# Six raw weight buffers, five pairs of split weights, and one look-ahead of five parts

## The chip, the cores and the metric

The kernel runs on one core of a Trainium2 chip. The metric is the device time of one execution in microseconds, as the median of several runs. Beside the times there is one profiled execution, with a row for every instruction and transfer.

## The reference

A decoder trunk of four layers on one sequence of 256 tokens of width 1024, in float32. Layer by layer the token mixer is native sparse attention (NSA), MoBA block attention, a short gated convolution, and NSA again; each layer ends in a SwiGLU feed-forward network with 2816 hidden columns.

```python
def swiglu(a, w_gate, w_up, w_down):
    return (jax.nn.silu(a @ w_gate) * (a @ w_up)) @ w_down

def reference(x, ...):
    h = x
    for i in range(DEPTH):                      # DEPTH = 4
        kind, j = i % N_MIXERS, i // N_MIXERS   # 0 NSA, 1 MoBA, 2 short conv
        a = rms_norm(h, norm_mix[i])
        m = ...mixer of this kind...
        h = h + m
        a = rms_norm(h, norm_ffn[i])
        h = h + swiglu(a, ffn_w_gate[i], ffn_w_up[i], ffn_w_down[i])
    return rms_norm(h, norm_final)
```

## The kernel before

All weight matrices lie in memory as one long stream of blocks, in the order of use. A block, called a part, is 128 partitions x 1024 values (512 KB): eight 128x128 tiles. SyncE issues the load of a part (L113) into a tile named raw, of which there are RAW_BUFS. TensorE multiplies at float32r precision, so each float32 operand is split in two: ScalarE casts raw to the high half (L167, whi), VectorE subtracts the high half from raw to get the low half (L171, wlo; in a few places GpSimd, called POOL, does it in four pieces), and the product is hi x hi + hi x lo + lo x hi. A pair of whi and wlo occupies one of W_BUFS slots until TensorE has done its last multiplication with it; a raw buffer is free when its subtraction is done. One raw buffer is 4 KB of each partition and one pair 8 KB.

`take` hands out tiles in the order of the stream. When it is called for a part, it first writes down the loads and splits of the parts ahead of it that have none yet. How far ahead is AHEAD = 5 parts, and one more where the part in hand belongs to the feed-forward network (names "ffn" and "fast"). A scheduler then sets the order of instructions on each engine, from the order in which they were written and from the buffers that they need; each engine works its own list strictly in order, and SyncE's list is also the queue of loads and moves. So an engine that waits for one thing holds up all that stands behind it in its list.

The hidden columns are made in groups of four 128-column tiles (g = 0, 4, 8, 12, 16, 20). An ordinary group multiplies eight parts (L461 to L463). Groups g = 8 and g = 16 of each layer are "fast": the first half of the inner dimension goes through seven block products in place of eight. Their operands are the blocks B11, B21, B22 and the sums T1 to T4, which VectorE makes in place in the blocks (L120); the loads are at L130, the splits at L134 (shi, ScalarE) and L135 (slo, VectorE). The seven products (L401 to L403) run in the order B11, T1, B21, T2, B22, T4, T3. The number behind shi and slo counts operands in the order of use; the number behind raw, whi and wlo is the part's place in memory.

ScalarE's copies (L412) of three of the partial results, named gu, ph and u2/u3 (tile pr), empty the banks for use again: u3 is the last, made when all seven products are done. Then four ordinary raw parts, k = 4 to 7, are multiplied (L435 to L437) on top, into the same banks. So the first matmul of L435 into u3's bank waits for u3's copy.

What a group leaves goes through `hidden`: silu on ScalarE (L360), a product (L361) and a transpose (L362) on VectorE, then `spread`: 16 moves from SBUF to SBUF on SyncE's queue (L376, four at a time, tied behind the newest weight load), a cast (L257, ScalarE) and a subtraction (L258, VectorE) for each of the four tiles. In a fast group these last two belong to the group before the previous one, and `hidden` to the previous one.

In attention, scores are exponentiated on ScalarE (L581), the reciprocal of their sum comes from VectorE (rc, L583), POOL scales by it (pr, L585), and TensorE transposes the result (L659 and L661 in MoBA).

Of the kernel before, what the change touches and what calls it, by code (L numbers as in the profile page):

```python
# [27 lines left out]
PART = 8  # L28
LAYERS = range(4)
AHEAD = 5  # L30
RAW_BUFS = 4
W_BUFS = 6
PR_BUFS = 4
MOVES = 4
FF_BUFS = 26
# [28 lines left out]
class Kernel:  # L64
# [44 lines left out]
    def load_part(self, q, cut=1):  # L109
        t = self.wp.tile([P, PART * P], F32, tag="raw", name=f"raw{q}", bufs=RAW_BUFS)  # L110
        n = PART * P // cut
        for i in range(cut):
            self.load = self.nc.sync.dma_start(t[:, i * n:(i + 1) * n], self.ap["w"][q, :, i * n:(i + 1) * n])  # L113
        self.raw[q] = t
# [8 lines left out]
    def fast_part(self, x):  # L123
# [7 lines left out]
        b = self.blocks  # L131
        hi = self.operands.tile([P, PART * P], F32R, tag="whi", name=f"shi{x}", bufs=W_BUFS)
        lo = self.operands.tile([P, PART * P], F32R, tag="wlo", name=f"slo{x}", bufs=W_BUFS)
        self.nc.scalar.copy(hi, b[what])  # L134
# [10 lines left out]
    def split_part(self, x):  # L145
# [5 lines left out]
        if self.names[q] == "F":  # L151
            t = self.operands.tile([P, PART * P], F32, tag="whi", name=f"wf{q}", bufs=W_BUFS)
            nc.sync.dma_start(t, self.ap["w"][q])
# [4 lines left out]
        src = self.raw.pop(q)  # L158
        hi = self.operands.tile([P, PART * P], F32R, tag="whi", name=f"whi{q}", bufs=W_BUFS)
        lo = self.operands.tile([P, PART * P], F32R, tag="wlo", name=f"wlo{q}", bufs=W_BUFS)  # L160
        lo_eng, hi_eng = (e.get(self.names[q], d) for e, d in ((LO, "v"), (HI, "a")))
# [12 lines left out]
    def take(self, n=1):  # L174

        q, o = divmod(self.pos, PART)
        assert o + n <= PART
        ahead = AHEAD + (self.names[self.seq[q][0]] in ("ffn", "fast"))
        for x in range(q, min(q + ahead, len(self.seq))):
            if x not in self.parts:  # L180
                self.split_part(x)
        while self.jobs and self.jobs[0][0] <= self.when[q]:
            self.jobs.pop(0)[1]()
        self.pos += n
        hi, lo = self.parts[q]
        return hi[:, o * P:(o + n) * P], lo[:, o * P:(o + n) * P]
# [836 lines left out]
    def run(self):  # L1023
# [8 lines left out]
        for k in range(0, KT, 2):  # L1032
            nc.sync.dma_start(x[:, k:k + 2, :], ap["xt"][:, k:k + 2, :])
            q = k // 4
            if k % 4 == 0:
                self.raw[q] = self.wp.tile([P, PART * P], F32, tag="raw", name=f"raw{q}", bufs=RAW_BUFS)
            c = slice(k % 4 // 2 * n, (k % 4 // 2 + 1) * n)
            nc.sync.dma_start(self.raw[q][:, c], ap["w"][q, :, c])
        for q in range(2, RAW_BUFS):
            self.load_part(q)  # L1040
# [148 lines left out]
```

## Time and profile before

| | before |
|---|---|
| median of 3 runs | 1254.41 us (1254.0 to 1258.1) |
| profiled execution | 1258.91 us, of which the span is 1257.1 us |
| mean granted TensorE clock | 0.992 |
| TensorE busy | 1222.2 us (97%) |
| VectorE busy | 972.3 us (77%) |
| ScalarE busy | 718.0 us (57%) |
| POOL busy | 296.5 us (24%) |
| read from memory | 213.33 MB, 171 GB/s over the span |

Rows of the profile give the start and length of an instruction, its engine (PE is TensorE, DVE VectorE, ACT ScalarE, SP SyncE), its line, and out<-in tiles with buffer numbers left out; "[2.83 <-DMA pt<-pt]" means that the engine was idle for 2.83 us just before and that a move ended the wait. A row of waits gives the total, the count and the longest. Matmul rows overlap, since TensorE is pipelined: their pace is the distance between starts, 0.23 us for 512 columns at the full clock.

### The profile page before, as it was taken

The page shows a single profiled execution, that of the slowest core. Times are in us where ns is not written, and L with a number is a line of the kernel's source. Part 1 is how long each engine was busy: PE and PEld are TensorE (multiplying, and loading weights), DVE is VectorE, ACT ScalarE, POOL GpSimd, SP SyncE. Part 2 cuts the span into 40 slices and gives each one's busy share as a digit, 9 for nine tenths or more (in the row PEclk, how much of TensorE's full clock was granted, in tenths as well). Part 3 has the DMA queues.
Part 4 walks back from the last instruction along what each step waited for, and adds up shares of the span by engine and source line. Part 5 has one row for each costly group of instructions (what it writes and reads, how often), then busy time and mean ns, then how long its engine had stood idle before and what let it go on. Part 6 is the DMA issues. An engine that isn't in the chain of part 4 may idle for free.

```text
span 1257.1 us, 19456 instructions
## 1 busy us (share of the span) xinstructions
PE 1222.2 (97%) x6740; PEld 1055.8 (84%) x6740; DVE 972.3 (77%) x1741; ACT 718.0 (57%) x1290; POOL 296.5 (24%) x405
## 2 busy tenths in 40 slices
PE   8998999999999899999999999999999999999997
PEld 7987888878899788888888888878899878888786
DVE  7779897975868688887778898775758798879653
ACT  5689655644456445655444556464536896566442
POOL 1077650100113442000123250000330776400000
PEclk9999999999999999999999999999999999999999
DMA  8742166567654436766765655566666422664672
GB/s 296 232 148 95 68 219 184 166 184 222 233 172 141 159 106 188 247 208 209 226 220 170 197 177 176 174 214 181 223 219 207 136 78 76 207 193 154 209 233 83
DMA packets 91587, 227.21 MB, mean 181 GB/s; under 512 B 17504, under 2 KB 38368, under 8 KB 91488
## 3 DMA queue, kind: packets, MB, share of 16 engines
q1 hardware_dynamic: 91056, 225.41, 56.9%
q8 instruction: 53, 0.87, 0.3%
q10 hardware_dynamic: 432, 0.56, 0.1%
q14 instruction: 46, 0.38, 0.1%
HBM read 213.33 MB, written 1.05 MB: 171 GB/s over the span
## 4 chain that ended last, share of the span: by engine, by line
PE 48%; DVE 9%; ACT 3%; issue 3%; POOL 2%; DMA 2%; SPq 1%; POOLq 0%; ACTq 0%; DVEq 0%
PE psA L218 8%; PE psA L222 4%; DVE wlo L171 3%; PE psB L461 2%; PE psB L463 2%; PE psB L462 2%; PE psA L461 2%; PE psA L463 2%; PE psA L462 2%; SPq L376 1%; PE psB L218 1%; DMA raw<-in_w 1%; ACT whi L167 1%; PE psB L782 1%; PE psA L198 1%
## 5 line engine op out<-in xcount | busy, mean ns | idle before, releaser
L171 DVE TENSOR_TENSOR wlo<-raw,whi 128x1024 fp32r<-128x1024 f32 (+1 forms) x334 | 411.3, 1249 | 139.8 <-ACT whi L167 134.2
L167 ACT CAST whi<-raw 128x1024 fp32r<-128x1024 f32 (+1 forms) x347 | 357.1, 1039 | 283.7 <-DMA raw<-in_w 188.0
L218 PE MATMUL psA<-ff,whi 128*128 128x512 f32 x686 | 182.2, 393 | 0.2 <-DVE row L989 0.2
L218 PEld LDWEIGHTS psA<-ff,whi 128*128 128x128 f32 x686 | 124.5, 189 | 23.0 <-DVE row L989 0.6
L198 PE MATMUL psA<-at,whi 128*128 128x256 f32 x352 | 102.1, 290 | 1.7 <-DVE row L548 1.7
L222 PE MATMUL psA<-ff,wlo 128*128 128x256 f32 x686 | 101.4, 283 | 0.0
L222 PEld LDWEIGHTS psA<-ff,wlo 128*128 128x128 f32 x686 | 96.1, 191 | 5.3
L200 PE MATMUL psA<-at,wlo 128*128 128x256 f32 x352 | 100.6, 286 | 0.0
L199 PE MATMUL psA<-at,whi 128*128 128x256 f32 x352 | 100.4, 285 | 0.0
L585 POOL TENSOR_SCALAR pr<-pr,rc,gates 128x256 f32<-128x256 f32 (+1 forms) x128 | 72.2, 580 | 118.7 <-DVE rc L583 116.5
L461 PE MATMUL psB<-whi,at 128*128 128x512 f32 x224 | 87.9, 392 | 0.6 <-ACT pr L360 0.6
L463 PE MATMUL psB<-whi,at 128*128 128x512 f32 x224 | 87.3, 390 | 0.0
L461 PE MATMUL psA<-whi,at 128*128 128x512 f32 x224 | 87.3, 390 | 0.0
L463 PE MATMUL psA<-whi,at 128*128 128x512 f32 x224 | 87.3, 390 | 0.0
L462 PE MATMUL psB<-wlo,at 128*128 128x512 f32 x224 | 87.2, 390 | 0.0
L462 PE MATMUL psA<-wlo,at 128*128 128x512 f32 x224 | 87.2, 389 | 0.0
L285 POOL TENSOR_TENSOR ssq<-ssq,row 128x256 f32<-128x256 f32 x42 | 38.7, 922 | 205.5 <-ACT row L283 143.1
L171 POOL TENSOR_TENSOR wlo<-raw,whi 128x256 fp32r<-128x256 f32 x96 | 74.7, 812 | 38.2 <-ACT whi L167 17.2
L134 ACT CAST shi<-B 128x1024 fp32r<-128x1024 f32 x56 | 57.8, 1049 | 37.3 <-DVE B L120 25.3
L581 ACT ACTIVATE pr<-pr,mn 128x128 f32<-128x128 f32 (+1 forms) x160 | 71.2, 447 | 7.2 <-DVE mn L578 6.7
L135 DVE TENSOR_TENSOR slo<-B,shi 128x1024 fp32r<-128x1024 f32 x56 | 66.8, 1217 | 8.1 <-ACT shi L134 8.1
L198 PEld LDWEIGHTS psA<-at,whi 128*128 128x128 f32 x352 | 68.1, 193 | 2.7 <-DVE row L548 2.5
(293 smaller groups left out, 2720.2 us busy)
## 6 DMA issues: line engine op xcount, KB each, us to landing
raw<-in_w SPq DMA_DIRECT2D x352, 512.0 KB, 4.3
B<-in_w SPq DMA_DIRECT2D x32, 512.0 KB, 3.8
pt<-pt SPq DMA_DIRECT2D x320, 32.0 KB, 2.7
wf<-in_w SPq DMA_DIRECT2D x16, 512.0 KB, 5.6
h<-in_xt SPq DMA_DIRECT2D x4, 256.0 KB, 5.3
raw<-in_w SPq DMA_DIRECT2D x4, 256.0 KB, 5.3
pt<-pt SPq DMA_DIRECT2D x64, 16.0 KB, 3.2
w<-in_w SPq DMA_DIRECT2D x2, 256.0 KB, 3.8
```

What stands on the lines that cost most here:

```text
L167: copy(hi[:, c], src[:, c])
L171: eng.tensor_tensor(out=lo[:, d], in0=src[:, d], in1=hi[:, d].bitcast(F32), op=OP.subtract)
L198: mm(out, wt[0], act[0], start=first, stop=False)
L199: mm(out, wt[0], act[1], start=False, stop=False)
L200: mm(out, wt[1], act[0], start=False, stop=last)
L218: mm(outs[o], w[0], acts[k].rearrange("p i s -> p (i s)"), start=(k == 0), stop=(k == n - 1))
L222: mm(outs[o][:, :S], w[1], acts[k][:, 0, :], start=False, stop=False)
L461: mm(o, a[:, 0, s], hi, start=(k == 0), stop=False)
L462: mm(o, a[:, 0, s], lo, start=False, stop=False)
L463: mm(o, a[:, 1, s], hi, start=False, stop=(k == KT - 1))
L581: nc.scalar.activation(pr[:, c], pr[:, c], AF.Exp, bias=mn[:, j:j + 1], scale=-1.0, accum_out=den[:, j:j + 1])
L585: getattr(nc, PR[j % len(PR)]).tensor_scalar(pr[:, c], pr[:, c], rc[:, j:j + 1], gates[j], op0=OP.mult, op1=OP.mult)
```

## The change

The look-ahead is five parts wherever `take` is called, also in the feed-forward network; two raw buffers are added, and one pair of split operands is taken away, so that the memory used stays the same.

```diff
 AHEAD = 5
-RAW_BUFS = 4
-W_BUFS = 6
+RAW_BUFS = 6
+W_BUFS = 5
...
         q, o = divmod(self.pos, PART)
         assert o + n <= PART
-        ahead = AHEAD + (self.names[self.seq[q][0]] in ("ffn", "fast"))
-        for x in range(q, min(q + ahead, len(self.seq))):
+        for x in range(q, min(q + AHEAD, len(self.seq))):
             if x not in self.parts:
                 self.split_part(x)
```

Behind this place every line number is smaller by one in the changed kernel: L412 becomes L411, L257 becomes L256.

Since a split is written down when its part comes within the look-ahead, the lists of all engines shift. Three places follow. First ScalarE in the second fast group of layer 3: the casts of the raw parts k = 4 to 7 are whi372 to whi375, whi376 is the next group's first, and pr_1340 and pr_1341 are u2 and u3. Before:

```order
L167 CAST whi372_12400<-raw372_12398 128x1024
L167 CAST whi373_12420<-raw373_12418 128x1024
L412 ACTIVATE pr_1340_12430<-psB_1334_12370,rstd_1273_11776 128x512
L167 CAST whi374_12434<-raw374_12432 128x1024
L167 CAST whi375_12446<-raw375_12444 128x1024
L167 CAST whi376_12458<-raw376_12456 128x1024
L412 ACTIVATE pr_1341_12472<-psB_1334_12370,rstd_1273_11776 128x512
L167 CAST whi377_12476<-raw377_12474 128x1024
```

After, in the same place:

```order
L167 CAST whi372_12414<-raw372_12412 128x1024
L411 ACTIVATE pr_1340_12424<-psB_1334_12366,rstd_1273_11770 128x512
L167 CAST whi373_12428<-raw373_12426 128x1024
L167 CAST whi374_12440<-raw374_12438 128x1024
L167 CAST whi375_12452<-raw375_12450 128x1024
L411 ACTIVATE pr_1341_12466<-psB_1334_12366,rstd_1273_11770 128x512
L167 CAST whi376_12470<-raw376_12468 128x1024
L167 CAST whi377_12488<-raw377_12486 128x1024
```

The copy of u3 stood behind the casts of five raw parts and now stands behind four.

Second, the first fast group of layer 3. On ScalarE, shi370 to shi372 are casts of the first three fast operands and L257 (L256) the casts of the four moved hidden tiles. Before:

```order
L134 CAST shi370_11860<-B11_1288_11852 128x1024
L134 CAST shi371_11882<-B11_1288_11852 128x1024
L134 CAST shi372_11903<-B21_1291_11858 128x1024
L257 CAST ff_1280_11790<-pt_1279_11789 128x256
L257 CAST ff_1281_11791<-pt_1279_11789 128x256
L257 CAST ff_1282_11792<-pt_1279_11789 128x256
L257 CAST ff_1283_11793<-pt_1279_11789 128x256
```

After:

```order
L134 CAST shi370_11876<-B11_1288_11868 128x1024
L256 CAST ff_1280_11784<-pt_1279_11783 128x256
L134 CAST shi371_11898<-B11_1288_11868 128x1024
L256 CAST ff_1281_11785<-pt_1279_11783 128x256
L256 CAST ff_1282_11786<-pt_1279_11783 128x256
L256 CAST ff_1283_11787<-pt_1279_11783 128x256
L134 CAST shi372_11919<-B21_1291_11874 128x1024
```

The casts of the moved tiles, which wait for the moves, now stand ahead of the second and third fast cast. On VectorE at the same place, before:

```order
L135 TENSOR_TENSOR slo372_11904<-B21_1291_11858,shi372_11903 128x1024
L258 TENSOR_TENSOR ff_1280_11790<-pt_1279_11789,ff_1280_11790 128x256
L120 TENSOR_TENSOR B21_1291_11858<-B21_1291_11858,B11_1288_11852 128x1024
L135 TENSOR_TENSOR slo373_11925<-B11_1288_11852,shi373_11924 128x1024
L258 TENSOR_TENSOR ff_1281_11791<-pt_1279_11789,ff_1281_11791 128x256
L258 TENSOR_TENSOR ff_1282_11792<-pt_1279_11789,ff_1282_11792 128x256
L258 TENSOR_TENSOR ff_1283_11793<-pt_1279_11789,ff_1283_11793 128x256
L135 TENSOR_TENSOR slo374_11945<-B22_1290_11856,shi374_11944 128x1024
L361 SCALAR_TENSOR_TENSOR pr_1294_11962<-psA_1285_11795,rstd_1273_11776,pr_1293_11961 128x512
L361 SCALAR_TENSOR_TENSOR pr_1296_11967<-psB_1287_11797,rstd_1273_11776,pr_1295_11966 128x512
```

After:

```order
L257 TENSOR_TENSOR ff_1280_11784<-pt_1279_11783,ff_1280_11784 128x256
L135 TENSOR_TENSOR slo371_11899<-B11_1288_11868,shi371_11898 128x1024
L257 TENSOR_TENSOR ff_1281_11785<-pt_1279_11783,ff_1281_11785 128x256
L120 TENSOR_TENSOR B11_1288_11868<-B22_1290_11872,B11_1288_11868 128x1024
L135 TENSOR_TENSOR slo372_11920<-B21_1291_11874,shi372_11919 128x1024
L257 TENSOR_TENSOR ff_1282_11786<-pt_1279_11783,ff_1282_11786 128x256
L120 TENSOR_TENSOR B21_1291_11874<-B21_1291_11874,B11_1288_11868 128x1024
L135 TENSOR_TENSOR slo373_11941<-B11_1288_11868,shi373_11940 128x1024
L360 SCALAR_TENSOR_TENSOR pr_1294_11958<-psA_1285_11789,rstd_1273_11770,pr_1293_11957 128x512
L135 TENSOR_TENSOR slo374_11977<-B22_1290_11872,shi374_11976 128x1024
```

The first of the moved tiles' subtractions stood behind slo371 and slo372 and now stands ahead of both; the hidden products (L361, now L360) are mixed with the last fast subtractions, slo374 to slo376.

Third, POOL in MoBA's softmax (layer 1): pr_531 and pr_549 are scaled scores of two heads' blocks, wlo129 and wlo131 low halves of weights. Before:

```order
L171 TENSOR_TENSOR wlo127_4693<-raw127_4690,whi127_4692 128x256 x4
L171 TENSOR_TENSOR wlo129_4781<-raw129_4778,whi129_4780 128x256 x3
L585 TENSOR_SCALAR pr_531_4671<-pr_531_4671,rc_534_4674 128x128 x2
L585 TENSOR_SCALAR pr_531_4671<-pr_531_4671,rc_534_4674 128x256 x2
L171 TENSOR_TENSOR wlo129_4781<-raw129_4778,whi129_4780 128x256
L171 TENSOR_TENSOR wlo131_5026<-raw131_5023,whi131_5025 128x256 x4
L585 TENSOR_SCALAR pr_549_4825<-pr_549_4825,rc_552_4828 128x128 x2
```

After:

```order
L171 TENSOR_TENSOR wlo127_4693<-raw127_4690,whi127_4692 128x256 x4
L584 TENSOR_SCALAR pr_531_4671<-pr_531_4671,rc_534_4674 128x128 x2
L584 TENSOR_SCALAR pr_531_4671<-pr_531_4671,rc_534_4674 128x256 x2
L171 TENSOR_TENSOR wlo129_4781<-raw129_4778,whi129_4780 128x256 x4
L584 TENSOR_SCALAR pr_549_4825<-pr_549_4825,rc_552_4828 128x128 x2
L584 TENSOR_SCALAR pr_549_4825<-pr_549_4825,rc_552_4828 128x256 x2
L171 TENSOR_TENSOR wlo131_5026<-raw131_5023,whi131_5025 128x256 x4
```

The scaling of pr_531 stood behind three pieces of wlo129 and now stands ahead of them, and pr_549 ahead of wlo131.

## The prediction

> **What bounds the kernel now.** I read the page first, then TensorE's waits, then the stretches where they lie, and last the chain of work that leads into one of them. From the page:
>
> ```profile
> PE 1222.2 (97%) x6740; PEld 1055.8 (84%) x6740; DVE 972.3 (77%) x1741; ACT 718.0 (57%) x1290; POOL 296.5 (24%) x405
> L171 DVE TENSOR_TENSOR wlo<-raw,whi 128x1024 fp32r<-128x1024 f32 (+1 forms) x334 | 411.3, 1249 | 139.8 <-ACT whi L167 134.2
> raw<-in_w SPq DMA_DIRECT2D x352, 512.0 KB, 4.3
> ```
>
> TensorE is busy 97% of the span. The change touches no arithmetic, so all it can win is TensorE's idle time and its slow stretches. A part's subtraction costs VectorE 1.25 us, and its load takes 4.3 us. TensorE's waits, longest first:
>
> ```profile
> PE psB L435 <- ACT pr L412: 7.2, 3, 2.7
> PE psA L246 <- ACT whi L167: 6.3, 1, 6.3
> PE psB L661 <- POOL pr L585: 2.9, 2, 1.4
> PE psB L659 <- POOL pr L585: 2.4, 2, 1.3
> ```
>
> Only one wait is for a split weight: the very first, before anything can be multiplied. Weights are otherwise in time. The three waits of the first row are the largest thing there is to win. They stand in the second fast group of layers 0, 2 and 3; the same group of layer 1 has none. Ten microseconds around each of the four, in the order of layers 0, 1, 2, 3 (columns: length, busy time of each engine with its count, the clock granted to TensorE, DMA share, GB/s):
>
> ```profile
> 253.00:263.00 10.00, 7.83 (x28) 6.01 (x27) 7.05 (x7) 4.19 (x5) 0.00 (x0) 0.83 0.82 241
> 556.00:566.00 10.00, 10.00 (x46) 8.28 (x45) 6.55 (x9) 4.87 (x6) 0.00 (x0) 1.00 0.82 281
> 828.00:838.00 10.00, 7.61 (x27) 5.83 (x26) 7.06 (x6) 3.89 (x5) 0.00 (x0) 0.83 0.80 246
> 1162.00:1172.00 10.00, 7.33 (x26) 5.56 (x25) 7.10 (x8) 4.38 (x5) 0.00 (x0) 0.83 0.84 243
> ```
>
> A pause is followed by a lower clock: 0.83 over 10 us, where layer 1 keeps 1.00, costs another 0.17 x 10 = 1.7 us. The chain in layer 3 (start, length, what):
>
> ```profile
> 1160.22 1.24 DVE wlo L171
> 1161.47 4.18 DMA raw<-in_w
> 1165.75 1.05 ACT whi L167
> 1166.80 0.59 ACT pr L412
> 1167.44 0.69 PE psB L435
> 1168.13 0.43 PE psB L436
> ```
>
> The fifth raw part of the look-ahead has no raw buffer until VectorE has finished with the first of the five (1161.46). Its load lands at 1165.65, and its cast stands on ScalarE ahead of u3's copy (L412), which empties the bank that TensorE waits for. That cast belongs to the next group and is wanted four parts later. In layer 1 the copy stands ahead of it:
>
> ```profile
> 559.53 0.69 ACT L412 ACTIVATE pr<-psB,rstd 128x512 f32<-128x512 f32 x1 [1.45 <-PE psB L403]
> ```
>
> There the copy waits for its own matmul, and TensorE does not stop.
>
> **The change part by part.** It adds and removes no matmul, cast, subtraction or load; it moves them.
>
> *Second fast groups: gain.* Two raw buffers more take away the wait for 1161.46: the fifth load can go out with the others. One part less of look-ahead puts u3's copy ahead of the fifth cast in all four layers. Either by itself breaks the chain, so the pauses should go: 7.2 us of waits and 3 x 1.7 = 5.1 us of clock, 12.3 us. What is late next is small: the copy now comes behind four casts of raw parts that are already there. Layer 1 shows that case with the copy in time. But VectorE's order also puts the hidden group's operations ahead of the last two fast subtractions, each of which takes 1.2 us. I price it from 0 to 1.0 us a group, take 0.2, and get 0.8 for four.
>
> *First fast groups: cost.* The look-ahead of five lets ScalarE meet the casts of the moved hidden tiles (L257) before the second fast cast; before, two or three fast casts stood ahead of them. In layer 3:
>
> ```profile
> 1102.51 1.06 ACT L134 CAST shi<-B 128x1024 fp32r<-128x1024 f32 x1 [0.76 <-PE psB L463]
> 1106.40 1.33 ACT L257 CAST ff<-pt 128x256 fp32r<-128x256 f32 x4 [2.83 <-DMA pt<-pt]
> 1101.78 1.23 DVE L135 TENSOR_TENSOR slo<-B,shi 128x1024 fp32r<-128x1024 f32 x1
> 1104.18 1.22 DVE L135 TENSOR_TENSOR slo<-B,shi 128x1024 fp32r<-128x1024 f32 x1
> 1108.71 1.23 DVE L135 TENSOR_TENSOR slo<-B,shi 128x1024 fp32r<-128x1024 f32 x1 [0.31 <-ACT shi L134]
> 1111.99 0.75 DVE L361 SCALAR_TENSOR_TENSOR pr<-psA,rstd,pr 128x512 f32<-128x512 f32 x1
> 1113.31 1.30 DVE L362 STREAM_TRANSPOSE pt<-pr 128x512 f32<-128x512 f32 x2
> 1114.53 2.32 DVE L135 TENSOR_TENSOR slo<-B,shi 128x1024 fp32r<-128x1024 f32 x2
> 1110.41 0.39 PE L401 MATMUL psB<-shi,at 128*128 128x512 f32 x1
> 1117.21 0.39 PE L401 MATMUL psA<-shi,at 128*128 128x512 f32 x1
> ```
>
> The moves land at 1106.4, and TensorE starts the first of seven products at 1110.41, a product every (1117.21 - 1110.41) / 5 = 1.36 us. Ahead of the landing VectorE did slo371, the sum T2 and slo372, from 1101.78 to 1105.4, 3.6 us; now they come behind it. I chain them: second cast done at 1107.8, slo371 to 1109.1, a move's subtraction and T2 to 1110.6, slo372 to 1111.8, a move's and T4 to 1113.35, slo373 to 1114.55, a hidden product (L361, 0.7), slo374 to 1116.45, a transpose and a product (1.3), slo375 to 1118.95, a transpose (0.65), slo376 to 1120.8 (a move's subtraction taken like its cast, 1.33 / 4). The sixth product wants its low half 0.23 us behind its start, at 1117.44, so it is 1.5 us late, and the seventh adds 0.5: 2.0 us. Before, the last two were done at 1116.8, which is the slack that it eats. In the other layers the gap between landing and first product decides (landing, then the product's start, layers 0, 1, 2):
>
> ```profile
> 198.05 1.33 ACT L257 CAST ff<-pt 128x256 fp32r<-128x256 f32 x4 [2.69 <-DMA pt<-pt]
> 202.21 0.39 PE L401 MATMUL psB<-shi,at 128*128 128x512 f32 x1
> 502.36 1.33 ACT L257 CAST ff<-pt 128x256 fp32r<-128x256 f32 x4 [1.56 <-DMA pt<-pt]
> 507.65 0.39 PE L401 MATMUL psB<-shi,at 128*128 128x512 f32 x1
> 769.29 1.33 ACT L257 CAST ff<-pt 128x256 fp32r<-128x256 f32 x4 [1.09 <-DMA pt<-pt]
> 776.86 0.39 PE L401 MATMUL psB<-shi,at 128*128 128x512 f32 x1
> ```
>
> 4.2, 5.3 and 7.6 us against 4.0 in layer 3: 2.0 us in layer 0, 0.8 in layer 1 (1.2 less), none in layer 2. Together 4.8 us. A lost clock could follow in layers 0 and 3, 1.7 us each; the pauses are scattered and shorter than the 2.4 us of the rows above, so I count 1.0. Bounds: 0, if moves land earlier, and 3 x 3.7 = 11.
>
> The Trainium skill ("TensorE: Matmul & The Clock Gate", Part 1) says that the clock is halved after an idle window of about 3.4 us. Here pauses of at most 2.7 us were each followed by matmuls 0.43 us apart, so the trace does not bear out that threshold; by the page the clock terms, 5.1 won and 1.0 lost, would both be zero.
>
> *MoBA's softmax: gain.* Layer 1's four waits for POOL (L585), 5.3 us:
>
> ```profile
> 414.55 2.13 POOL L171 TENSOR_TENSOR wlo<-raw,whi 128x256 fp32r<-128x256 f32 x3 [7.67 <-PE psA L200]
> 416.66 3.28 POOL L585 TENSOR_SCALAR pr<-pr,rc 128x128 f32<-128x128 f32 x4
> 414.91 0.18 DVE L583 RECIPROCAL rc<-den 128x4 f32<-128x4 f32 x1
> 417.77 0.33 PE L659 MATMUL psB<-ident,pr 128*128 128x128 f32 x1 [1.09 <-POOL pr L585]
> 419.54 0.33 PE L661 MATMUL psB<-ident,pr 128*128 128x128 f32 x1 [1.44 <-POOL pr L585]
> ```
>
> The reciprocal is there at 415.1, but three pieces of a subtraction hold POOL to 416.66. They now stand behind, so the transposes come up to 1.5 us sooner each time. Two later reciprocals lose 0.3 to 0.8 us to splits placed ahead of them. I take 2.5 us of gain, from 0 to 4. NSA's softmax keeps its pattern with casts shifted by a part: 0, within 2 either way.
>
> *One pair fewer.* A cast of part x now waits for the end of x-5. Even now casts wait for TensorE to give back a slot, and no wait of TensorE comes of it:
>
> ```profile
> ACT whi L167 <- PE psA L218: 17.0, 10, 3.4
> ```
>
> An ordinary part takes TensorE as long as two products, 2.7 us, more than cast (1.05) plus subtraction (1.25), so five pairs keep up. Cost 0, at most 2 where VectorE is also busy. The start has two more loads ahead of small ones and two subtractions among the sums of squares: 0.4, from 0 to 1.
>
> *Sum:* -12.3 + 0.8 + 4.8 + 1.0 - 2.5 + 0.4 = -7.8 us. The profiled execution took 1258.91 us and would take 1251.1; it is 4.5 us above the median of the runs, 1254.41, which therefore becomes 1246.6.
>
> **The rivals.**
> - *The first fast groups lose nothing* (moves land earlier, or VectorE catches up). For it: the first product starts 4 us behind the landing. Against it: 3.6 us of VectorE's work moved behind the landing. 1254.4 - 12.3 - 2.5 = 1239.6.
> - *It cancels.* The first fast groups of layers 0, 1 and 3 stop 2 us and lose the clock too (3 x 3.7 = 11.1), the second ones 0.5 each (2.0): -14.8 + 13.1, 1252.7.
> - *The slow matmuls do not come from the pauses* but recur at those places. Then the clock terms fall away: -7.2 + 0.8 + 4.8 - 2.5 + 0.4 = -3.7, 1250.7. Against it: 0.83 in the three groups with a pause, 1.00 in the one without. That is how the time comes out by the page on the clock gate.
> - *Slower.* VectorE, with one pair fewer, has no lead when it enters any of the eight fast groups, and each stops for 2.0 us with its clock gone: 8 x 3.7 = 29.6 against 14.8 won, 1269. It decides where a fast group costs over 14.8 / 8 = 1.85 us. For it: in layer 3 VectorE's rows from 1108.71 to 1116.8 leave it little idle time. Against it: landing gaps of 5.3 and 7.6 us in layers 1 and 2.
>
> **How the numbers follow.** Forecast case 0.55, nothing lost 0.20, cancels 0.10, slow matmuls of their own 0.06, slower 0.09. About 0.3% (3.8 us, so 1250.6 and 1258.2) can be told from no change. Faster: 0.50 + 0.20 + 0.04 = 0.74; the same: 0.05 + 0.09 + 0.01 = 0.15; slower: 0.09 + 0.01 + 0.01 = 0.11. The range leaves out part of the best case and the slower one: 1239 to 1257, which also takes in the bounds of the first fast groups (0 to 11 us).
>
> **What would show it.** Right: no wait on L411 (L412 before) at the second fast groups, granted clock 1.00 there, a first product of MoBA's transposes without POOL ahead of it, and waits of 0.5 to 1.5 us of the products on slo in the first fast groups of layers 0 and 3. Wrong: pauses that stay at the second fast groups (then neither buffers nor order were their cause), or waits on slo or wlo over 2 us in all eight groups.

## The result, and the profile after

The changed kernel takes 1245.72 us (median of 6 runs, 1243.08 to 1246.46) against 1255.3 us before (6 runs, 1253.67 to 1258.1): a ratio of 0.9918, 95% interval 0.9903 to 0.9934, or 9.6 us less. Taken again on another occasion it gave 1243.92 us and 0.9913 (0.9892 to 0.9933). Forecast were 1246.6 us. The profiled execution took 1243.98 us, 14.9 us less than the profiled one of before. This gap is the larger one because the profiled execution of before was 3.6 us slower than the median of its kernel, and that of the changed kernel 1.7 us faster than its own.

The first line of the page after, with the busy time of each engine:

```profile
PE 1215.8 (98%) x6740; PEld 1050.3 (85%) x6740; DVE 971.4 (78%) x1741; ACT 717.6 (58%) x1290; POOL 282.0 (23%) x405
```

The instructions are the same in number. The mean granted clock rose from 0.992 to 0.997: 0.008 x 1257.1 less 0.003 x 1242.2 is 6.3 us of the 14.9. Those of TensorE's waits after that bear on the change (total, count, longest):

```profile
PE psA L245 <- ACT whi L167: 6.1, 1, 6.1
PE psB L460 <- DVE pr L441: 3.3, 4, 1.4
PE psA L197 <- DVE row L547: 2.1, 2, 1.4
PE psB L461 <- DVE wlo L171: 1.0, 2, 0.5
PE psB L660 <- POOL pr L584: 0.7, 2, 0.5
PE psB L658 <- POOL pr L584: 0.7, 1, 0.7
```

The 7.2 us for u3's copy are gone. MoBA's waits for the scaling fell from 5.3 to 1.4 us. New are 3.3 us for L441, the add behind a fast group that empties a bank, in four places, and 1.0 us for a late low half in the first group of a feed-forward network. The second fast groups of layers 0 to 3 (columns as in the table before):

```profile
248.00:258.00 10.00, 10.00 (x46) 8.28 (x45) 10.00 (x12) 8.46 (x11) 3.13 (x6) 1.00 0.52 165
544.00:554.00 10.00, 10.00 (x46) 8.27 (x45) 10.00 (x11) 8.45 (x11) 0.00 (x0) 1.00 0.69 229
818.00:828.00 10.00, 10.00 (x46) 8.29 (x45) 9.12 (x11) 7.17 (x9) 0.00 (x0) 1.00 0.57 146
1148.00:1158.00 10.00, 10.00 (x46) 8.24 (x44) 9.99 (x11) 7.21 (x10) 0.00 (x0) 1.00 0.52 122
```

TensorE is busy all through, at the full clock. Here is the chain of work that leads into the second longest wait for L441, in layer 3:

```profile
1119.65 0.24 PE psB L436
1119.91 1.06 ACT whi L167
1120.99 1.23 DVE wlo L171
1122.22 0.67 DVE pr L441
1122.93 0.50 PE psB L460
```

The fast group's last matmuls into the bank are done before 1120, but the add that empties it waits on VectorE behind a subtraction, whose cast was late. Why it was late shows on SyncE's queue in the changed kernel (start, length, count) and in ScalarE's rows of the part before it and of this one:

```profile
1106.38 6.08 SPq L375 DMA_DIRECT2D pt<-pt  x8
1112.56 0.53 SPq L113 DMA_DIRECT2D raw<-in_w  x1
1113.13 2.50 SPq L375 DMA_DIRECT2D pt<-pt  x4
1115.73 0.53 SPq L113 DMA_DIRECT2D raw<-in_w  x1
1117.15 1.05 ACT L167 CAST whi<-raw 128x1024 fp32r<-128x1024 f32 x1 [4.34 <-DMA raw<-in_w]
1119.91 1.05 ACT L167 CAST whi<-raw 128x1024 fp32r<-128x1024 f32 x1 [1.71 <-PE psB L436]
```

The load of raw362 stands behind eight moves, is issued at 1112.56 and lands at 1117.1; ScalarE waits 4.34 us for it. The cast in the chain is the next one, of raw363, whose load stands behind four more moves, is issued at 1115.73 and takes 4.1 us. The profile puts the end of this cast's wait down to a matmul (L436) that ended at the same moment. But with five pairs the cast takes the slot of the part five before it, and TensorE was done with that part one part (2.7 us) earlier, so it is the load that came last.

A sum over the whole trace says the same in one number: for every matmul the distance to the start of the next, less the median distance for the same line and width, summed in stretches of 50 us. It is TensorE's lost time, idle and slow clock together, on one profiled execution of each kernel; "MoBA" is the stretch from 400 to 450 us. RAW, W and A stand for raw buffers, pairs, and the look-ahead in the feed-forward network; the column of the other fast places is the four first fast groups with the group behind each. The totals and the MoBA column move by 1 to 2 us with the way in which the usual distance is taken, and differences to the row of before come out larger here than between the medians, as they do between the two profiled executions.

| kernel | RAW, W, A | lost in all, us | second fast groups | MoBA | other fast places |
|---|---|---|---|---|---|
| before | 4, 6, 6 | 46.9 | 13.4 | 9.1 | 0 |
| changed | 6, 5, 5 | 32.1 | 0 | 2.7 | 5.3 |
| look-ahead alone | 4, 6, 5 | 45.0 | 0 | 9.1 | 11.0 |
| buffers alone | 6, 5, 6 | 27.7 | 0.2 | 2.8 | 1.0 |
| look-ahead and pairs | 4, 5, 5 | 34.9 | 3.5 | 2.9 | 4.6 |
| pairs alone | 4, 5, 6 | 33.9 | 0 | 2.6 | 7.3 |

### The profile page after: what moved, and what is told of

It reads as the page before. It is cut to its first block, busy times and chain, and to the rows that moved or that the text cites. A ratio compares the mean times of both kernels' runs of the same rounds, so it can differ in the third digit from the quotient of the medians.

```text
span 1242.2 us, 19453 instructions
## 1 busy us (share of the span) xinstructions
PE 1215.8 (98%) x6740; PEld 1050.3 (85%) x6740; DVE 971.4 (78%) x1741; ACT 717.6 (58%) x1290; POOL 282.0 (23%) x405
## 4 chain that ended last, share of the span: by engine, by line
PE 73%; DVE 12%; ACT 4%; issue 3%; SPq 3%; POOL 3%; DMA 2%; POOLq 0%; ACTq 0%; DVEq 0%
PE psA L217 13%; PE psA L221 7%; DVE wlo L171 4%; PE psB L460 3%; PE psB L461 3%; PE psB L462 3%; PE psA L460 3%; PE psA L462 3%; PE psA L461 3%; SPq L375 3%; PE psA L197 2%; PE psB L781 2%; PE psA L198 2%; PE psA L199 2%; PE psB L217 2%
## 5 line engine op out<-in xcount | busy, mean ns | idle before, releaser
L461 PE MATMUL psB<-wlo,at 128*128 128x512 f32 x224 | 87.4, 390 | 1.0 <-DVE wlo L171 1.0
L461 PE MATMUL psA<-wlo,at 128*128 128x512 f32 x224 | 87.2, 389 | 0.0
L284 POOL TENSOR_TENSOR ssq<-ssq,row 128x256 f32<-128x256 f32 x42 | 34.2, 813 | 208.9 <-ACT row L282 152.2
L171 POOL TENSOR_TENSOR wlo<-raw,whi 128x256 fp32r<-128x256 f32 x96 | 69.4, 758 | 38.1 <-ACT whi L167 18.1
```

The costliest lines, as they stand in the source:

```text
L171: eng.tensor_tensor(out=lo[:, d], in0=src[:, d], in1=hi[:, d].bitcast(F32), op=OP.subtract)
L461: mm(o, a[:, 0, s], lo, start=False, stop=False)
```

## The experiments

**Which of the three edits does what.** Four kernels on one chip, against a median of 1252.52 us of the kernel before there.

*The look-ahead alone.*

```diff
-        ahead = AHEAD + (self.names[self.seq[q][0]] in ("ffn", "fast"))
-        for x in range(q, min(q + ahead, len(self.seq))):
+        for x in range(q, min(q + AHEAD, len(self.seq))):
```

> Look-ahead of five everywhere, four raw buffers and six pairs as before. Theory A (at the second fast groups u3's copy only has to stand ahead of the fifth raw part's cast, or that part's load has to have a buffer; either is enough): here the copy stands behind four casts, so the three pauses of 2.2 to 2.4 us and the slow clock behind them are gone, about 12 us; MoBA's softmax stays as before (its POOL order is that of before, waits on L584 of about 5 us), since that part comes from the pairs; the waits on L441 of the changed kernel (3.3 us) are not there, since with six pairs the cast that holds VectorE up is earlier. 1242 to 1248. Rival B (the buffers are what mattered): the fifth load still waits for a buffer and the pauses stay, 1252 to 1256.

Measured: 1255.99 us, ratio 1.0022 (1.0009 to 1.0036). Neither theory foresaw it. The second fast groups run without a pause, as theory A says, but the pause has moved to the first fast group of all four layers. TensorE's wait, and ScalarE in the first fast group of layer 3:

```profile
PE psB L434 <- ACT pr L411: 8.1, 4, 2.9
1114.07 1.99 ACT L167 CAST whi<-raw 128x1024 fp32r<-128x1024 f32 x2
1120.74 1.04 ACT L167 CAST whi<-raw 128x1024 fp32r<-128x1024 f32 x1 [4.68 <-DMA raw<-in_w]
1121.69 0.68 ACT L411 ACTIVATE pr<-psB,rstd 128x512 f32<-128x512 f32 x1
```

There the shorter look-ahead put the fifth raw part's cast ahead of u3's copy, where it had stood behind it before. It is the same chain in another place: a cast that waits for its load, with a copy behind it that TensorE needs. The mechanism holds, but a shorter look-ahead is no remedy for it.

*The buffers alone.*

```diff
-RAW_BUFS = 4
-W_BUFS = 6
+RAW_BUFS = 6
+W_BUFS = 5
```

> Six raw buffers and five pairs, the look-ahead of before (six in the feed-forward network). u3's copy stands behind five casts, as before. Theory A: the fifth load has a buffer, so its cast does not wait, and the copy is at most one cast (1 us) later than in the changed kernel: no wait on L412 over 0.7 us at the second fast groups, clock 1.00 there; MoBA gains as in the changed kernel (waits on L585 under 2 us); waits on L442 (the adds that empty banks behind the first fast groups) of 3 to 5 us as in the changed kernel. 1244 to 1250. Rival C (only the place of the copy matters): pauses of over 1 us in three of the four second fast groups, 1250 to 1256.

Measured: 1239.62 us, ratio 0.9898 (0.9883 to 0.9914), better than foreseen, and better than the changed kernel's 0.9918 and 0.9913. u3's copy stands behind five casts, just as before, and this is ScalarE in the second fast group of layer 3:

```profile
1144.61 0.71 ACT L412 ACTIVATE pr<-psB,rstd 128x512 f32<-128x512 f32 x1
1145.19 3.18 ACT L167 CAST whi<-raw 128x1024 fp32r<-128x1024 f32 x3
1148.28 0.69 ACT L412 ACTIVATE pr<-psB,rstd 128x512 f32<-128x512 f32 x1
```

The loads are there, the casts run back to back, and the copy is in time: rival C is out. The waits on L442 that I expected here too are missing, though VectorE's list puts the same subtraction ahead of the add. So that order and the five pairs alone do not make them.

*Look-ahead and pairs*, with four raw buffers (RAW_BUFS = 4 in the changed kernel).

> The changed kernel with four raw buffers in place of six: look-ahead five, five pairs. Its order of instructions puts u3's copy behind four casts, MoBA's scaling ahead of the split, and the two adds that empty banks behind the first fast groups (L441) ahead of the next subtraction. Theory A: the two raw buffers were not needed; all gains of the changed kernel stay and its waits on L441 (3.3 us) go: 1239 to 1244. Rival B (the buffers are what mattered): loads are late, pauses stay or casts wait for loads: 1250 to 1256.

Measured: 1247.56 us, ratio 0.9963 (0.9949 to 0.9977). Between the theories: MoBA gains and of the waits on L441 only 0.2 us are left, but 3.5 and 4.6 us are lost in the fast groups, among others in waits on slo (1.0 us) and on gu's copy (0.8 us).

*Pairs alone* (W_BUFS = 5, all else as before).

> Five pairs in place of six, all else as before. The order of instructions puts u3's copy ahead of the fifth cast here too, because that cast now needs a slot that is given back later. Theory A: the pauses at the second fast groups go, MoBA gains, no waits on L442: 1239 to 1246. Rival D (one pair fewer takes weights' lead away): waits of TensorE on wlo and slo of 1 us or more in the fast groups, 1250 or more. Rival B: pauses stay, 1250 to 1256.

Measured: 1244.28 us, ratio 0.9934 (0.9921 to 0.9948). Taking away one pair of buffers, and nothing else, is worth 8 us. The pauses go because u3's copy now stands ahead of the fifth cast: in layer 3 the copy starts at 1154.39 and that cast at 1157.11. That the scheduler chose this order because the cast's slot is given back later is argued and not shown. But waits on L442 are there, where I expected none, though the add stands ahead of the next subtraction here. TensorE's wait, and ScalarE ahead of the one in layer 1:

```profile
PE psB L461 <- DVE pr L442: 3.2, 3, 1.4
519.49 2.00 ACT L167 CAST whi<-raw 128x1024 fp32r<-128x1024 f32 x2 [2.77 <-DMA raw<-in_w]
```

Again two casts that waited for a load, and behind their subtractions the add: with four raw buffers loads are late here, too.

Read together: one pair fewer is worth 8 us (1252.5 to 1244.3 us, and 1256.0 to 1247.6 with the short look-ahead). Two raw buffers more are worth another 4.7 (1244.3 to 1239.6). The short look-ahead costs 3.3 to 3.5 us with four raw buffers; with six, the next four kernels show it. No run has six raw buffers with six pairs, so what the buffers are worth without the pair taken away is not known.

**Why the short look-ahead costs.** If it is the load behind eight moves, the place of the moves must decide, not the lead of the weights. Four kernels on one chip, against 1253.82 us of the kernel before.

> The changed kernel once more, on the chip of the three beside it. 1243 to 1247; waits on L441 of 3 to 4 us in four places, as in its first profile.

Measured: 1243.92 us, with 3.9 us of waits on L441 in four places.

*The moves one part later*, all else as in the changed kernel:

```diff
-            spread(turned, n, 3)
+            spread(turned, n, 4)
```

> The changed kernel, with the moves of an ordinary group's hidden tiles written down one part later (spread's third argument 4 in place of 3 in hidden). On SyncE's queue the load of the seventh raw part behind the first fast group (raw362 in layer 3) then stands behind one batch of four moves, not behind two. Theory E (the look-ahead of five costs what it does because that load is issued about 2.5 us later behind eight moves, its cast and its subtraction follow late, and the add that empties a bank stands behind them on VectorE): waits on L441 from 3.3 to under 1 us, 1240 to 1243. Rival F (a look-ahead of five simply gives weights less lead): waits on L441 and the time stay, 1244 to 1247.

Measured: 1240.19 us, ratio 0.9886 (0.9866 to 0.9905). No wait on L441 is left. SyncE's queue at the place that the changed kernel showed above:

```profile
1103.36 2.52 SPq L375 DMA_DIRECT2D pt<-pt  x4
1105.97 1.15 SPq L113 DMA_DIRECT2D raw<-in_w  x1
1107.16 2.51 SPq L375 DMA_DIRECT2D pt<-pt  x4
```

Four moves, the load, four moves: with the look-ahead still at five, 3.7 us are back by the order of SyncE's queue alone.

*Look-ahead six in one half of the feed-forward network* (both with six raw buffers and five pairs; the names in the test of `take` are "fast" alone, then "ffn" alone).

> Six raw buffers, five pairs, look-ahead six in the parts of the fast groups only, five in the ordinary groups. The load of raw362 stands behind one batch of four moves. Theory E: no waits on L442, 1238 to 1241, as the run with buffers alone. Rival F: between that run and the changed kernel, since half of the feed-forward network has the shorter lead: 1242 to 1244, with waits on wlo.

> The other half: look-ahead six in the ordinary groups, five in the fast ones. The load of raw362 stands behind eight moves, as in the changed kernel. Theory E: waits on L442 of 3 us or so stay, 1243 to 1247. Rival F: 1241 to 1243, half of the loss is back.

Measured: 1240.06 us, ratio 0.9885 (0.9863 to 0.9907), no wait on L442; and 1243.08 us, 0.9909 (0.9889 to 0.9928), with

```profile
PE psB L461 <- DVE pr L442: 3.5, 4, 1.4
```

All as theory E has it: only the half that puts the load behind four moves helps.

*The moves one part earlier* (spread's argument 2), twelve moves ahead of the load; on a chip where the kernel before took 1254.5 us.

> The changed kernel with the moves written down one part earlier (spread's third argument 2 in hidden): the load of raw362 stands behind three batches, twelve moves. Theory E, as a dose: with four, eight and twelve moves ahead the waits on L441 are 0, 3.9 and, with 2.5 us more in each of four places, 8 to 14 us, with the clock behind them: 1250 to 1260. Rival F (lead of the weights): no more than now, 1243 to 1246.

Measured: 1251.52 us, ratio 0.9973 (0.9959 to 0.9986). The wait grows with the moves ahead of the load, as theory E says, but less than I summed:

```profile
PE psB L460 <- DVE pr L441: 6.5, 4, 2.1
PE psA L401 <- DVE slo L135: 1.4, 3, 0.7
```

0, 3.9 and 6.5 us with four, eight and twelve moves. The waits on slo, 1.4 us, are not among the changed kernel's. A sum over the trace as in the table puts 9.6 us into the first fast places and 1.8 us into the second fast groups, against 6.0 and 0 in the second profile of the changed kernel; that is 5.4 of the 5.9 us between these two profiled executions.

**Where MoBA's gain comes from.** In the table all kernels with five pairs lose 2.6 to 2.9 us there, both with six pairs 9.1. I put it down to POOL, which scaled scores behind pieces of a subtraction. The test takes those subtractions off POOL, in the kernel before:

```diff
-LO = {"nsa_out": "p", "moba_out": "vp", "A": "p", "F": "ppv"}
+LO = {"nsa_out": "p", "moba_out": "v", "A": "p", "F": "ppv"}
```

> The kernel before, with the low halves of MoBA's output weights made on VectorE only, none on POOL. Theory G (MoBA's gain of 6 us comes from POOL: the scaling of scores, L585, no longer stands behind pieces of wlo129 and wlo131): waits on L585 in MoBA fall from 5.3 to under 2.5 us, though VectorE has four subtractions more; the pauses at the second fast groups stay; 1247 to 1251, against 1252 to 1255 of the kernel before. Rival H (the gain comes of VectorE's order, casts of weights that no longer stand ahead of the reciprocals): no gain, 1252 to 1257.

Measured: 1253.66 us, ratio 0.9993 (0.9978 to 1.0007): no difference that can be told. POOL, the reciprocal and TensorE there:

```profile
413.57 0.18 DVE L583 RECIPROCAL rc<-den 128x4 f32<-128x4 f32 x1
413.94 4.29 POOL L585 TENSOR_SCALAR pr<-pr,rc 128x128 f32<-128x128 f32 x4 [16.97 <-DVE rc L583]
416.82 0.33 PE L661 MATMUL psB<-ident,pr 128*128 128x128 f32 x1 [1.36 <-POOL pr L585]
414.12 1.26 DVE L171 TENSOR_TENSOR wlo<-raw,whi 128x1024 fp32r<-128x1024 f32 x1
416.68 1.21 DVE L171 TENSOR_TENSOR wlo<-raw,whi 128x1024 fp32r<-128x1024 f32 x1
```

POOL scales at once when the reciprocal is there, as theory G has it, and TensorE waits all the same: the waits on L585 fell only from 5.3 to 4.4 us. But the test does not decide against G. The four scalings took 3.28 us before and take 4.29 us here, where VectorE runs two subtractions beside them, one of which POOL would have done before. So the edit may have taken back on one side what it gave on the other; that the subtractions are what lengthens the scalings is not shown by itself. In the changed kernel the reciprocal is there sooner, and the scalings are shorter:

```profile
410.04 0.18 DVE L582 RECIPROCAL rc<-den 128x4 f32<-128x4 f32 x1 [0.16 <-ACT pr L580]
410.31 2.31 POOL L584 TENSOR_SCALAR pr<-pr,rc 128x128 f32<-128x128 f32 x4 [2.45 <-DVE rc L582]
```

The reciprocal comes at 410.04 against 414.91 us before. TensorE's 2381st matmul starts 3.2 us sooner (409.53 against 412.68), so 1.7 us of this are the reciprocal's own. Counted from that matmul, the four scalings end 4.2 us sooner than before: 1.7 us by the reciprocal, 1.5 us because no pieces of wlo129 stand between it and the scaling, and 1.0 us because the scalings are shorter. The 1.7 us can be read from VectorE's list. Before, an add (L682) and the cast whi129, which waits for TensorE, stand just ahead of the reciprocal:

```profile
413.72 0.69 DVE L167 CAST whi<-raw 128x1024 fp32r<-128x1024 f32 x1 [0.50 <-PE psA L199]
```

In the changed kernel both stand behind it. That agrees with rival H. The test says nothing of H, since in it the cast still stood ahead of the reciprocal. So the trace of the changed kernel has a share for each theory, and no run separates them.

The same edit on six raw buffers, five pairs and look-ahead six:

> Six raw buffers, five pairs, look-ahead as before (six in the feed-forward network), and MoBA's low halves on VectorE only. The remaining waits on L585 in MoBA (1.4 us) and VectorE's extra work decide: 1237 to 1242, with 1239.6 for the same without the last edit.

Measured: 1244.28 us, ratio 0.9912 (0.9894 to 0.9931), outside what I wrote and worse than without it (1239.62 us). The profile loses 8.1 us in MoBA, in place of 2.8, and the four scalings take 4.28 us there too. POOL's subtractions there are better left where they are.

**One step further**: eight raw buffers and four pairs, look-ahead as before.

> One step further the same way: eight raw buffers, four pairs, look-ahead as before. Theory D (a pair is worth nothing until splits come late): with four pairs a cast waits for the end of the part four back, 10.9 us ahead of its use, and in the fast groups half of that; waits on wlo and slo of 1 to 2 us in several places, and twelve moves stand ahead of the load of raw364: 1245 to 1262. Rival: buffers of loads are what counts, 1236 to 1240.

Measured: 1264.43 us, ratio 1.0077 (1.0059 to 1.0095). The loss is spread: 51.6 us in all, 10.6 of it in MoBA, where the order of before is back (a cast ahead of the reciprocal, three pieces of wlo129 ahead of the scaling), and up to 2.2 in a fast group. So fewer pairs are not better as such; five happens to give a good order.

## Why the prediction was right, point by point

- *Second fast groups, 12.3 us won.* Right in place and mechanism: 13.4 us lost before, none after; the 0.8 us counted against it for the later copy did not come. "Either by itself breaks the chain" was half right. Six raw buffers do it everywhere, with five pairs. The look-ahead alone breaks it there and makes it anew in the first fast groups, which I had not followed; and one pair fewer moves the copy too.
- *First fast groups, 4.8 us and 1.0 us of clock lost.* This step failed. I moved the casts and left the moves' landing where it was. But the hidden transposes moved as well: one subtraction (1.2 us) less stands ahead of them on VectorE, and the moves are issued earlier. SyncE's first row of these moves before, and then, of the changed kernel, the moves, the cast, the first product of layer 3 and the subtraction for the last one:

```profile
1094.61 1.87 SPq L376 DMA_DIRECT2D pt<-pt  x3
...
1081.98 10.18 SPq L375 DMA_DIRECT2D pt<-pt  x16
1093.69 0.41 ACT L256 CAST ff<-pt 128x256 fp32r<-128x256 f32 x1 [4.34 <-DMA pt<-pt]
1098.97 0.39 PE L400 MATMUL psB<-shi,at 128*128 128x512 f32 x1
1106.24 1.18 DVE L135 TENSOR_TENSOR slo<-B,shi 128x1024 fp32r<-128x1024 f32 x1
```

  The moves start 17.0 us ahead of the first product, in place of 15.8 (1110.41 - 1094.61), and the landing has a lead of 5.3 us, in place of 4.0: 1.3 us. The chain from the landing to the last subtraction took 13.7 us (1107.42 - 1093.69), where I had added up 14.4 (1120.8 - 1106.4): another 0.7. My chain ended 2.0 us late, so the two cancel it, and no wait for slo is among TensorE's waits, where I had named 0.5 to 1.5 us as a sign. It was the rival "nothing lost", here. I also named the wrong edit: in the kernels' orders the casts of the moved tiles come forward with one pair fewer, not with the look-ahead.
- *What took its place.* Waits of 3.3 us on L441 one group later, none of which I had. They come from SyncE's queue: I looked at the casts and subtractions that moved and not at where the loads stand among the moves. The first fast places, with the group behind each, lose 5.3 us in all, about the 4.8 and 1.0 us in error, so this part of the sum came out right by two errors that cancel, which is luck.
- *MoBA, 2.5 us won, from 0 to 4.* Waits fell by 3.9 us, and the lost time by 6.4, which is over the range. Before, the granted clock from 420 to 430 us was 0.83, and it is 1.00 after: 1.7 us for which I had no term. The cause that I gave, POOL's pieces ahead of the scaling, is 1.5 us at the first reciprocal; the earlier reciprocal (1.7) and the shorter scalings (1.0) were not in it.
- *One pair fewer, 0.* Late low halves cost 1.0 us of waits in two places (L461), within the bound of 2. As a change of order it was worth 8 us.
- *The start, 0.4.* The stretch up to 50 us loses 2.5 us against 2.2, and the first matmul starts 0.2 us sooner.
- *The sum, -7.8 us.* It was built on the profiled execution, and between the two profiled ones the time fell by 14.9 us: 1.9 us more than forecast at the second fast groups, 3.9 more in MoBA, and 0.5 less lost at the first ones. The median came within 0.9 us of 1246.6 because the two profiled executions lie on opposite sides of their medians. So the direction and the largest term were foreseen, and the closeness of the number is in part luck.
- *The rivals.* "Cancels" and "slower" did not come; the eight fast places lose 5.3 us together, 0.7 each, and the latter decides at 1.85. The slow matmuls do come with pauses, but not with each, as the last section shows.

The version that beats both kernels is any of three that keep six raw buffers and five pairs and leave the load behind four moves: 1239.62, 1240.06 and 1240.19 us.

## What to carry to other kernels

A buffer count and a look-ahead are also orders: where a scheduler lists instructions by when their buffers come free, each such number shifts every engine's list, and that was worth more here than the space itself (one pair fewer won 8 us). Look for the instruction that waits for a far-off load and has behind it, on the same engine, a small copy that TensorE needs; give the load a buffer, since moving the copy in one place can put it wrong in another. When you forecast such a shift, follow the queue that issues the transfers too, and shift the sources of a wait along with its users.

## What the runs showed of the hardware

A pause of TensorE of 2 to 3 us does not always cost its clock. Ten microseconds around four such pauses, the first two in the kernel with the look-ahead alone (after idle 2.56 and 2.86 us), the last two in the one with MoBA's split on VectorE (2.18 and 2.39 us):

```profile
212.00:222.00 10.00, 7.44 (x33) 5.83 (x32) 5.00 (x5) 3.88 (x5) 0.00 (x0) 1.00 0.80 257
1118.00:1128.00 10.00, 7.14 (x24) 5.38 (x24) 4.52 (x4) 3.71 (x4) 0.00 (x0) 0.83 0.80 241
825.00:835.00 10.00, 7.82 (x28) 5.97 (x27) 6.16 (x6) 3.96 (x5) 0.00 (x0) 0.83 0.86 250
1158.00:1168.00 10.00, 7.61 (x34) 5.99 (x33) 6.05 (x6) 4.26 (x5) 0.00 (x0) 1.00 0.83 243
```

2.18 us lost the clock, 2.39 and 2.56 did not, 2.86 did. In the profiled execution of before all three pauses lost it (2.17, 2.39 and 2.67 us).

The granted clock of the traces shows what decides. In the profiled execution of before it is half the full one for 3.41 us each from 259.64, 420.07, 833.08, 1024.23 and 1167.59 us on; three of these stretches:

```profile
259.64:263.05 3.41, 3.41 (x10) 2.67 (x9) 2.20 (x2) 1.68 (x2) 0.00 (x0) 0.50 0.80 217
420.07:423.48 3.41, 3.41 (x18) 3.41 (x18) 1.36 (x3) 1.16 (x3) 0.56 (x1) 0.50 0.41 129
833.08:836.49 3.41, 3.36 (x8) 2.68 (x9) 1.89 (x2) 1.91 (x2) 0.00 (x0) 0.50 0.83 269
```

The distances from one start to the next are 47, 121, 56 and 42 times 3.413 us, so the slow stretches begin on a fixed grid, and every other trace with more than one of them agrees. In the fast groups what counts is TensorE's idle time between two neighbouring points of that grid. It was 2.03, 2.34 and 2.67 us before the slow stretches of the kernel before, and 2.18 and 2.68 us in the two kernels above. The two pauses that kept the clock lie across a point of the grid, which leaves at most 1.52 of 2.56 us and 1.89 of 2.39 us on one side. So in these traces 2.03 us and more cost the clock there, and 1.89 us and less did not. In attention less idle time came ahead of a slow stretch (1.1 us at 1018.77 us with the moves one part earlier), so idle time is not all that counts there.

A kernel with the same pauses therefore loses its clock in some executions and keeps it in others. For eleven executions of the kernel before, beside the second set of the changed one, the granted clock was recorded as 0.990 to 0.999, and the two at these ends took 1259.97 and 1250.04 us. The medians are 0.994 before and 0.997 after, so about 3.8 of the 9.9 us between the two medians of time are clock, against 6.3 of 14.9 us between the two profiled executions.

The Trainium skill ("TensorE: Matmul & The Clock Gate", Part 1) says that the activity window of some 3.4 us runs freely and does not start anew with a kernel. The grid agrees with that, and so does the length of the slow stretches, 3.41 us. That the pause itself must fill a window is not borne out.
